# Pinning the modulation's products on VectorE and loading their rows one place ahead

## The chip, the cores and the metric

The kernel runs on one core of a Trainium2 chip. The metric is device time in microseconds (us): the median of three runs, and beside it one profiled execution from which all rows below come. Engines: TensorE (PE, matrix products; PEld its weight loads), VectorE (DVE), ScalarE (ACT), GpSimd (POOL) and SyncE (SP), whose queue issues the loads.

## The reference

Two layers of a hybrid trunk. 384 tokens (128 of a context pass, 256 of a denoising step) of width 1024 go through the same weights; each group has its own modulation vector. Per layer:

```
m   = silu(cvec) @ w_ada + b_ada            # 9 rows of 1024: shift, scale, gate for 3 sub-layers
ffn: h = rms_norm(x) * (1 + scale) + shift
     x = x + 0.5 * gate * ((silu(h @ wg) * (h @ wu)) @ wd)        # d_ff 2816
mixer: four head groups (windowed attention, a gated scan, latent attention, pooling) on one input
     projection, one output projection, x = x + gate * (...)
ffn again
```

A last rms_norm over x is the output y. All is float32.

## The kernel before, in words

The tokens lie along the free axis: x is eight tiles of 128 x 384 (k = 0 to 7). Every float32 weight tile is split into a high and a low half (`split_w`, L196 to L202): ScalarE copies the rounded high half (`higu`, `hidn`), VectorE subtracts it and leaves the low half (`logu`, `lodn`). A product is three TensorE instructions (`mm3`, L207 to L212): high weights with the high half of the input, high weights with its low half, and third, low weights with its high half. So TensorE needs the low half of a weight tile from its third instruction on.

An ffn (`ffn`, L299) goes through 38 places in a fixed order: 11 gate-and-up places (numbers 0 to 10; 48 products, or 24 for the gate and 24 for the up columns), 8 down places (11 to 18; 33 products each: 18 with the first 768 columns, 15 with the other 640), and the same again for the second half of d_ff (19 to 29, 30 to 37). At the end of a gate-and-up place VectorE multiplies `u` (gate times up, L336) and leaves its low half `al`; at the end of a down place it adds the result into x (`add_x`, L294, two instructions, one for each token group) and, in the second half, prepares the next sub-layer (`scaled`, L262, low half `hl`). The PSUM tag "d" has two banks, so x or u of a place must be read before the next but one can begin. Weights come by `load_w` (L121 to L125) into a pool of five buffers of 512 KB ("raw"): a load waits until a buffer's reader is done, and SyncE issues its loads in order.

The modulation rows are work on the side. The table SIDE says in which places a row n of layer l is worked out; a row is eight units (k = 0 to 7), spread over its places, so that where it has fewer places than units some places take two. Most run on VectorE (`ada_dve`, L167): a unit loads 512 KB of w_adaT and multiplies it in four instructions of 128 x 512 with the two modulation vectors, each leaving a sum (`accum_out`; the product itself goes to a PSUM tile named junk and is never read). One row (layer 0, n = 2) runs on TensorE (`ada_pe`, L143), in places 4 to 9 of the first ffn. `f()` of `side` (L1061) steps these generators once per place, behind the place's own code.

The code does not fix the order on an engine: a scheduler sets it from data dependences and its own estimates, and may move an instruction ahead of others. `tc.keep_in_program_order` pins one: it stays behind all that the program has before it on that engine, while later instructions that are not pinned may still move ahead of it. Each engine then executes its list in order.

At the end, `Sumsq` (L225) holds the sum of squares: with `apart` the last k is kept out of the running sum and added by a second product on TensorE; Ln and Exp on ScalarE make rstd, VectorE makes y and SyncE sends it (L1100 to L1107).

Of the kernel before, what the change touches and what calls it, by code (L numbers as in the profile page):

```python
# [7 lines left out]
F32 = mybir.dt.float32  # L8
F32R = mybir.dt.float32r
U8 = mybir.dt.uint8  # L10
AF = mybir.ActivationFunctionType
ALU = mybir.AluOpType
# [3 lines left out]
P = 128  # L16
D = 1024
KD = D // P
TP, TS = 128, 256
T = TP + TS  # L20
# [24 lines left out]
def trunk(ctx, tc, a):  # L45
    nc = tc.nc
# [8 lines left out]
    def nm(s):  # L55
        cnt[0] += 1
        return f"{s}_{cnt[0]}"
# [5 lines left out]
    def bank(s):  # L63
        return ps.tile([P, 512], F32, tag="b", name=nm(s), bufs=2)
# [4 lines left out]
    def xbank(s):  # L69
        return ps.tile([P, 2, 512], F32, tag="xb", name=nm(s), bufs=1)  # L70
# [50 lines left out]
    def load_w(src, s):  # L121
        t = sb.tile([P, 1024], F32, tag="raw", name=nm("raw" + s), bufs=5)
        n = src.shape[-1]
        nc.sync.dma_start(out=t[:, :n], in_=src)
        return t[:, :n]  # L125
# [29 lines left out]
    requests = {}  # L155
# [11 lines left out]
    def ada_dve(l, n):  # L167

        sums = sb.tile([P, KD, 2, 2], F32, tag="adasum", name=nm("adasum"), bufs=2)
        for k in range(KD):  # L170
            t = load_w(a["w_adaT"][l, n, k], "ada")
            for v in range(2):
                for z in range(2):
                    V.scalar_tensor_tensor(xbank("junk")[:, 0, :], t[:, z * 512:(z + 1) * 512], 1.0, requests[v, z],  # L174
                                           op0=ALU.mult, op1=ALU.mult, accum_out=sums[:, k, v, z:z + 1])
            if k == KD - 1:
                m = mods[l][:, n * 8:(n + 1) * 8, :]
                V.tensor_tensor(m, sums[:, :, :, 0], sums[:, :, :, 1], op=ALU.add)
                V.tensor_tensor(m, m, bada[:, l, n * 8:(n + 1) * 8].unsqueeze(2).to_broadcast([P, KD, 2]), op=ALU.add)
            yield  # L180
# [35 lines left out]
        V.tensor_tensor(lo, src, hi, op=ALU.subtract)  # L216


    def rstd_of(dst, acc, n):

        S.activation(dst, acc, AF.Ln, bias=epsb, scale=1.0 / n)
        S.activation(dst, dst, AF.Exp, scale=-0.5)
        return dst

    class Sumsq:  # L225
# [5 lines left out]
        def add(self, k):  # L231
            if self.n == 0:
                self.acc = one("ssq")
                S.activation(self.acc, x[k], AF.Square)
            else:
                sq = one("sq")
                S.activation(sq, x[k], AF.Square)  # L237
                if self.n < KD - self.apart:
                    (V if self.n == KD - 1 else G).tensor_tensor(self.acc, self.acc, sq, op=ALU.add)  # L239
                self.last = sq  # L240
            self.n += 1

        def end(self):
            b = bank("ms")
            PE.matmul(b[:, :T], ones, self.acc, start=True, stop=not self.apart)
            if self.apart:
                PE.matmul(b[:, :T], ones, self.last, start=False, stop=True)
            return rstd_of(sb.tile([P, T], F32, tag="rstd", name=nm("rstd"), bufs=1), b[:, :T], D)

    def log_exp():  # L250
        tc.keep_in_program_order(S.preload_act_table_set(LOGEXP))
# [39 lines left out]
                                   op0=ALU.add, op1=ALU.subtract)  # L291
        return t[:, 0, :], t[:, 1, :]

    def add_x(k, b, gt):  # L294
        for g, cs in GROUPS:
            V.scalar_tensor_tensor(x[k][:, cs], b[:, cs], gt[:, k, g:g + 1], x[k][:, cs], op0=ALU.mult, op1=ALU.add)  # L296


    def ffn(l, i, rstd, ab, nxt, side, hook=None, given=(), h=None):  # L299


        side = side()
        gt = None
        ssq = Sumsq(int(l == NL - 1 and i == 1))
        h = [None] * KD if h is None else h

        for half in range(2):
            act = []
            for fi in range(HF):
                f = half * HF + fi  # L310
                early = f < (5 if given else 4)
                order = [(z, k) for z in range(2) for k in range(KD)]
                if f < len(given):
                    (bg, bu), order = given[f], []
                else:
                    w = [weights(a["w_gu"][l, i, f, :, z * D:(z + 1) * D], "gu") for z in range(2)]
                    bg, bu = dbank("g"), dbank("u")
                if f == 0:
                    order.sort(key=lambda zk: zk[1])
                for z, k in order:  # L320
                    mm3((bg, bu)[z][:, :NX if early else T], w[z], k * P,
                        (hh[:, k, :], hl[:, k, :]) if early else h[k], k == 0, k == KD - 1)
                g, u = one("g"), one("u")
                if early:
                    sh = tiny("s", "sh", 2)
                    normed(g, bg, rstd, AF.Silu)
                    V.tensor_copy(sh, bu[:, T:NX])
                    V.tensor_tensor(u, bu[:, :T], rstd, op=ALU.mult)
                    for q, cs in GROUPS:
                        V.scalar_tensor_tensor(u[:, cs], u[:, cs], sh[:, q:q + 1], g[:, cs], op0=ALU.add, op1=ALU.mult)  # L330
                    for k in range((2 if given else f) * KD // 4, (f + 1) * KD // 4):
                        if k < KD and h[k] is None:
                            h[k] = hidden(k, ab, rstd)
                else:
                    S.activation(g, bg[:, :T], AF.Silu)  # L335
                    V.tensor_tensor(u, g, bu[:, :T], op=ALU.mult)  # L336
                if fi % 2 == 0:
                    ah = slot("H", "ah", (2, T), dt=F32R)
                    al = slot("H", "al", (2, T), dt=F32R)
                act.append((ah[:, fi % 2, :], al[:, fi % 2, :]))  # L340
                split_act(u, *act[-1])
                if f == NF - 1:
                    log_exp()
                if hook and f == 6:
                    hook()
                side()
            if gt is None:
                gt = gate(l, 2 * i)
            for j in range(KD):
                b = dbank("dn")  # L350
                fi = 0
                for z, n in ((0, 6), (1, 5)):
                    src = a["w_dn"][l, i, half, j]
                    w = weights(src[:, :6 * P] if z == 0 else src[:, 6 * P:], "dn")
                    for o in range(n):
                        mm3(b[:, :T], w, o * P, act[fi], fi == 0, fi == HF - 1)
                        fi += 1
                add_x(j, b, gt)
                if half == 1:
                    nxt(j)  # L360
                    ssq.add(j)
                side()
        return ssq
# [684 lines left out]
    def side(units):  # L1048

        places = [[] for _ in range(NF + 2 * KD)]  # L1050
        for by, l, n, p0, p1 in units:
            g = (ada_pe if by == "PE" else ada_dve)(l, n)
            for k in range(KD):
                places[p0 + k * (p1 + 1 - p0) // KD].append(g)
            if by == "PE":
                places[p1 + 1].append(g)
        first = min([NF] + [u[3] for u in units if u[0] == "DVE"])
        places[max(first - 2, 0)].insert(0, requests_of())
        todo = iter(places)

        def f():  # L1061
            for g in next(todo):
                next(g)
        return f
# [3 lines left out]
    def coefs_of(l, s):  # L1068
        if (l, s) not in coefs:
            coefs[l, s] = coef(l, s)  # L1070
        return coefs[l, s]

    def before(l, s):

        def f(j):
            if l < NL:
                at, bt = coefs_of(l, s)
                if j == 0:
                    shift(bt)
                scaled(j, at)  # L1080
        return f
# [7 lines left out]
    for l in range(NL):  # L1089
        if l > 0:  # L1090
            rstd = ssq.end()
            act_table(AF.Silu)
            ssq = ffn(l, 0, rstd, coefs_of(l, 0), before(l, 1), lambda: side(SIDE[2]))
        gt = gate(l, 1)
        rstd = ssq.end()
        act_table(AF.Sigmoid)
        ssq = mixers(l, rstd, gt, coefs_of(l, 1), before(l, 2))
        rstd = ssq.end()
        act_table(AF.Silu)
        ssq = ffn(l, 1, rstd, coefs_of(l, 2), before(l + 1, 0), lambda: side(SIDE[2 * l + 1]))  # L1100
    rstd = ssq.end()
    for k in range(KD):
        if k % 2 == 0:
            y = slot("M", "y", (2, T))
        V.scalar_tensor_tensor(y[:, k % 2, :], x[k], fnorm[:, k:k + 1], rstd, op0=ALU.mult, op1=ALU.mult)
        if k % 2 == 1:
            nc.sync.dma_start(out=a["o_y"][:, k - 1:k + 1, :], in_=y)  # L1107


_OUTS = {  # L1110
# [146 lines left out]
```

## Time and profile before

| | |
|---|---|
| median of 3 runs | 1548.63 us (1545.83 to 1549.92) |
| profiled execution | 1549.54 us, span 1547.8 us |
| TensorE busy | 1508.8 us, 97% |
| VectorE busy | 1177.6 us, 76% |
| modulation products on VectorE | 480, 339.8 us |
| bytes moved | 257.34 MB |

The span runs from the first instruction to the last. Products on TensorE are pipelined: they start 0.17 us apart while each lasts 0.34. "Idle before" is the time in which an engine did nothing before an instruction, and the arrow names what ended it. The granted clock of a stretch is 1.00 where TensorE had 2.4 GHz all through it and 0.50 at 1.2 GHz.

### The profile page before, as it was taken

To read this page: it belongs to the slowest core of one execution; us is meant where nothing else is said; L and a number is where in the kernel's file an instruction comes from. 1 tells how busy PE (TensorE), PEld (TensorE's weight loads), DVE (VectorE), ACT (ScalarE), POOL (GpSimd) and SP (SyncE) were. 2 spreads that over 40 slices of the span, in tenths; PEclk is the share of its full clock that TensorE was granted. 3 is DMA by queue.
4 is the path that set the end of the run, shared out by engine and by line. 5 is a ranking of instruction groups with operands and counts; after the bars stand their busy time and mean duration, and the time that the engine had idled before them with its cause. 6 is when DMAs were issued, how large, how long until landed. Compare 5 with 4: busy or idle time off the path is not lost.

```text
span 1547.8 us, 26740 instructions
## 1 busy us (share of the span) xinstructions
PE 1508.8 (97%) x10120; PEld 1426.4 (92%) x10120; DVE 1177.6 (76%) x2633; ACT 765.9 (49%) x1373; POOL 98.6 (6%) x122
## 2 busy tenths in 40 slices
PE   7999999999999999999999999999999999999997
PEld 5999999997778999999989999999877799999996
DVE  5889999969947988987977798785896599444433
ACT  6732333456788732333465323345677875323331
POOL 1000000101311000000100000001014010000001
PEclk9999999999999999999999999999999999999998
DMA  9777765642134465765654576555221156444331
GB/s 371 267 243 226 249 224 192 211 143 61 44 104 148 160 199 185 244 222 173 194 161 157 178 233 228 179 168 163 80 64 54 61 176 196 124 146 146 112 102 61
DMA packets 83026, 257.34 MB, mean 166 GB/s; under 512 B 9680, under 2 KB 11184, under 8 KB 82512
## 3 DMA queue, kind: packets, MB, share of 16 engines
q1 hardware_dynamic: 81744, 254.14, 50.5%
q8 instruction: 80, 1.31, 0.3%
q0 software_dynamic: 1152, 1.48, 0.3%
q14 instruction: 50, 0.41, 0.1%
HBM read 252.53 MB, written 2.26 MB: 165 GB/s over the span
## 4 chain that ended last, share of the span: by engine, by line
PE 70%; DVE 17%; DMA 6%; issue 3%; ACT 3%; SPq 0%; DVEq 0%; ACTq 0%
PE u L210 20%; PE g L210 19%; PE dn L210 12%; PE in L210 8%; DVE junk L174 5%; PE out L210 3%; DMA rawada<-in_w_adaT 3%; DVE lodn L201 2%; DMA rawgu<-in_w_gu 2%; DVE logu L201 2%; PE po L430 1%; DVE x L296 1%; PE sc L397 1%; DVE hl L265 1%; PE first L210 1%
## 5 line engine op out<-in xcount | busy, mean ns | idle before, releaser
L174 DVE SCALAR_TENSOR_TENSOR junk<-rawada,req 128x512 f32<-128x512 f32 x480 | 339.8, 708 | 31.1 <-DMA rawada<-in_w_adaT 20.9
L200 ACT ACTIVATE higu<-rawgu 128x1024 fp32r<-128x1024 f32 (+1 forms) x178 | 186.5, 1050 | 314.2 <-PE u L210 106.5
L210 PE MATMUL g<-h,higu 128*128 128x384 f32 x1136 | 291.6, 336 | 2.3 <-ACT g L335 2.2
L210 PE MATMUL u<-h,higu 128*128 128x384 f32 x1136 | 289.3, 334 | 2.3 <-DVE x L296 2.2
L201 DVE TENSOR_TENSOR logu<-rawgu,higu 128x1024 fp32r<-128x1024 f32 (+1 forms) x178 | 215.5, 1211 | 39.4 <-PE g L210 23.6
L210 PE MATMUL dn<-ah,hidn 128*128 128x384 f32 x704 | 236.1, 335 | 0.4 <-ACT hh L264 0.4
L210 PE MATMUL dn<-al,hidn 128*128 128x384 f32 x704 | 236.0, 335 | 0.0
L210 PE MATMUL dn<-ah,lodn 128*128 128x384 f32 x704 | 236.0, 335 | 0.0
L200 ACT ACTIVATE hidn<-rawdn 128x768 fp32r<-128x768 f32 (+1 forms) x128 | 101.3, 792 | 253.7 <-PE dn L210 70.1
L210 PEld LDWEIGHTS g<-h,higu 128*128 128x128 f32 x1136 | 205.7, 189 | 6.4 <-ACT g L335 3.1
L210 PEld LDWEIGHTS u<-h,higu 128*128 128x128 f32 x1136 | 204.9, 188 | 3.3 <-issue 1.5
L210 PE MATMUL g<-h,logu 128*128 128x384 f32 x568 | 190.6, 335 | 0.0
L210 PE MATMUL u<-h,logu 128*128 128x384 f32 x568 | 189.8, 334 | 0.0
L201 DVE TENSOR_TENSOR lodn<-rawdn,hidn 128x768 fp32r<-128x768 f32 (+1 forms) x128 | 113.4, 886 | 30.4 <-issue 17.0
L210 PEld LDWEIGHTS dn<-ah,hidn 128*128 128x128 f32 x704 | 132.1, 188 | 0.7 <-ACT hh L264 0.7
L210 PEld LDWEIGHTS dn<-ah,lodn 128*128 128x128 f32 x704 | 132.1, 188 | 0.0
L210 PEld LDWEIGHTS dn<-al,hidn 128*128 128x128 f32 x704 | 132.1, 188 | 0.0
L239 POOL TENSOR_TENSOR ssq<-ssq,sq 128x384 f32<-128x384 f32 x42 | 46.3, 1102 | 1155.5 <-ACT sq L237 658.0
L336 DVE TENSOR_TENSOR u<-g,u 128x384 f32<-128x384 f32 x71 | 39.2, 552 | 91.5 <-PE u L210 91.5
L210 PE MATMUL in<-hh,hiin 128*128 128x386 f32 x304 | 107.7, 354 | 0.0
L210 PEld LDWEIGHTS g<-h,logu 128*128 128x128 f32 x568 | 107.1, 189 | 0.0
L210 PEld LDWEIGHTS u<-h,logu 128*128 128x128 f32 x568 | 106.6, 188 | 0.0
(316 smaller groups left out, 2509.6 us busy)
## 6 DMA issues: line engine op xcount, KB each, us to landing
rawgu<-in_w_gu SPq DMA_DIRECT2D x170, 512.0 KB, 4.2
rawada<-in_w_adaT SPq DMA_DIRECT2D x120, 512.0 KB, 3.7
rawdn<-in_w_dn SPq DMA_DIRECT2D x64, 384.0 KB, 3.5
rawdn<-in_w_dn SPq DMA_DIRECT2D x64, 320.0 KB, 2.9
rawin<-in_w_in SPq DMA_DIRECT2D x38, 512.0 KB, 3.6
rawout<-in_w_out SPq DMA_DIRECT2D x32, 256.0 KB, 2.6
ada<-in_w_ada SPq DMA_DIRECT2D x16, 384.0 KB, 7.2
rawada<-in_w_ada SPq DMA_DIRECT2D x8, 512.0 KB, 4.9
```

What stands on the lines that cost most here:

```text
L174: V.scalar_tensor_tensor(xbank("junk")[:, 0, :], t[:, z * 512:(z + 1) * 512], 1.0, requests[v, z], op0=ALU.mult, op1=ALU.mult, accum_out=s ...
L200: S.activation(hi, raw, AF.Copy)
L201: V.tensor_tensor(lo, raw, hi, op=ALU.subtract)
L210: i = PE.matmul(out, wt, xt, start=first and n == 0, stop=last and n == 2)
L239: (V if self.n == KD - 1 else G).tensor_tensor(self.acc, self.acc, sq, op=ALU.add)
L265: V.scalar_tensor_tensor(hl[:, k, cs], x[k][:, cs], at[:, k, g:g + 1], hh[:, k, cs], op0=ALU.mult, op1=ALU.subtract)
L296: V.scalar_tensor_tensor(x[k][:, cs], b[:, cs], gt[:, k, g:g + 1], x[k][:, cs], op0=ALU.mult, op1=ALU.add)
L336: V.tensor_tensor(u, g, bu[:, :T], op=ALU.mult)
L397: PE.matmul(sc[:, u, :nk], q_of(u, blk), k_of(u, blk), start=True, stop=True)
L430: PE.matmul(bo[64 * u:64 * u + 64, :P], v_of(u, kt), pt[:, u, i * P:(i + 1) * P], start=(i == 0), stop=(i == len(kts) - 1))
```

## The change

In `ada_dve` the four products of a unit are pinned, and the load of unit k + 1 is issued in the code of unit k; the first unit issues two loads. At the end of the kernel the last x, its square, the sum, Ln, Exp and the first pair of y are worked out by column groups, 256 columns first and then 128, with Ln and Exp pinned; y takes its tiles from another pool, and its transfers go out on the queues of SyncE and ScalarE in turn, the last pair as two single tiles.

```diff
--- before.py
+++ after.py
@@ -167,12 +167,15 @@
     def ada_dve(l, n):
 
         sums = sb.tile([P, KD, 2, 2], F32, tag="adasum", name=nm("adasum"), bufs=2)
+        loads = [load_w(a["w_adaT"][l, n, 0], "ada")]
         for k in range(KD):
-            t = load_w(a["w_adaT"][l, n, k], "ada")
+            if k + 1 < KD:
+                loads.append(load_w(a["w_adaT"][l, n, k + 1], "ada"))
+            t = loads[k]
             for v in range(2):
                 for z in range(2):
-                    V.scalar_tensor_tensor(xbank("junk")[:, 0, :], t[:, z * 512:(z + 1) * 512], 1.0, requests[v, z],
-                                           op0=ALU.mult, op1=ALU.mult, accum_out=sums[:, k, v, z:z + 1])
+                    tc.keep_in_program_order(V.scalar_tensor_tensor(xbank("junk")[:, 0, :], t[:, z * 512:(z + 1) * 512], 1.0, requests[v, z],
+                                           op0=ALU.mult, op1=ALU.mult, accum_out=sums[:, k, v, z:z + 1]))
             if k == KD - 1:
                 m = mods[l][:, n * 8:(n + 1) * 8, :]
                 V.tensor_tensor(m, sums[:, :, :, 0], sums[:, :, :, 1], op=ALU.add)
@@ -216,10 +219,11 @@
         V.tensor_tensor(lo, src, hi, op=ALU.subtract)
 
 
-    def rstd_of(dst, acc, n):
-
-        S.activation(dst, acc, AF.Ln, bias=epsb, scale=1.0 / n)
-        S.activation(dst, dst, AF.Exp, scale=-0.5)
+    def rstd_of(dst, acc, n, pinned=False):
+
+        keep = tc.keep_in_program_order if pinned else lambda i: i
+        keep(S.activation(dst, acc, AF.Ln, bias=epsb, scale=1.0 / n))
+        keep(S.activation(dst, dst, AF.Exp, scale=-0.5))
         return dst
 
     class Sumsq:
@@ -234,18 +238,24 @@
                 S.activation(self.acc, x[k], AF.Square)
             else:
                 sq = one("sq")
-                S.activation(sq, x[k], AF.Square)
+                for _, cs in reversed(GROUPS) if self.apart and self.n == KD - 1 else ((0, slice(0, T)),):
+                    S.activation(sq[:, cs], x[k][:, cs], AF.Square)
                 if self.n < KD - self.apart:
                     (V if self.n == KD - 1 else G).tensor_tensor(self.acc, self.acc, sq, op=ALU.add)
                 self.last = sq
             self.n += 1
 
         def end(self):
-            b = bank("ms")
-            PE.matmul(b[:, :T], ones, self.acc, start=True, stop=not self.apart)
-            if self.apart:
-                PE.matmul(b[:, :T], ones, self.last, start=False, stop=True)
-            return rstd_of(sb.tile([P, T], F32, tag="rstd", name=nm("rstd"), bufs=1), b[:, :T], D)
+            rstd = sb.tile([P, T], F32, tag="rstd", name=nm("rstd"), bufs=1)
+            groups = GROUPS[::-1] if self.apart else ((0, slice(0, T)),)
+            bs = [bank("ms") for _ in groups]
+            for b, (_, cs) in zip(bs, groups):
+                PE.matmul(b[:, cs], ones, self.acc[:, cs], start=True, stop=not self.apart)
+            for b, (_, cs) in zip(bs, groups):
+                if self.apart:
+                    PE.matmul(b[:, cs], ones, self.last[:, cs], start=False, stop=True)
+                rstd_of(rstd[:, cs], b[:, cs], D, self.apart)
+            return rstd
 
     def log_exp():
         tc.keep_in_program_order(S.preload_act_table_set(LOGEXP))
@@ -291,8 +301,8 @@
                                    op0=ALU.add, op1=ALU.subtract)
         return t[:, 0, :], t[:, 1, :]
 
-    def add_x(k, b, gt):
-        for g, cs in GROUPS:
+    def add_x(k, b, gt, order=GROUPS):
+        for g, cs in order:
             V.scalar_tensor_tensor(x[k][:, cs], b[:, cs], gt[:, k, g:g + 1], x[k][:, cs], op0=ALU.mult, op1=ALU.add)
 
 
@@ -355,7 +365,7 @@
                     for o in range(n):
                         mm3(b[:, :T], w, o * P, act[fi], fi == 0, fi == HF - 1)
                         fi += 1
-                add_x(j, b, gt)
+                add_x(j, b, gt, GROUPS[::-1] if ssq.apart and half == 1 and j == KD - 1 else GROUPS)
                 if half == 1:
                     nxt(j)
                     ssq.add(j)
@@ -1098,13 +1108,17 @@
         rstd = ssq.end()
         act_table(AF.Silu)
         ssq = ffn(l, 1, rstd, coefs_of(l, 2), before(l + 1, 0), lambda: side(SIDE[2 * l + 1]))
+
     rstd = ssq.end()
-    for k in range(KD):
-        if k % 2 == 0:
-            y = slot("M", "y", (2, T))
-        V.scalar_tensor_tensor(y[:, k % 2, :], x[k], fnorm[:, k:k + 1], rstd, op0=ALU.mult, op1=ALU.mult)
-        if k % 2 == 1:
-            nc.sync.dma_start(out=a["o_y"][:, k - 1:k + 1, :], in_=y)
+    y = [slot("H", "y", (2, T)) for _ in range(KD // 2)]
+    for n, cs in ((0, GROUPS[1][1]), (0, GROUPS[0][1]), *((n, slice(0, T)) for n in range(1, KD // 2))):
+        for k in (2 * n, 2 * n + 1):
+            V.scalar_tensor_tensor(y[n][:, k % 2, cs], x[k][:, cs], fnorm[:, k:k + 1], rstd[:, cs],
+                                   op0=ALU.mult, op1=ALU.mult)
+            if n == KD // 2 - 1:
+                (nc.scalar, nc.sync)[k % 2].dma_start(out=a["o_y"][:, k, :], in_=y[n][:, k % 2, :])
+        if n < KD // 2 - 1:
+            (nc.sync, nc.scalar)[n % 2].dma_start(out=a["o_y"][:, 2 * n:2 * n + 2, cs], in_=y[n][:, :, cs])
 
 
 _OUTS = {
```

What the scheduler made of it is shown at two places. The first is VectorE in the first down-projection of layer 0 (places 11 to 18). `x<-dn_...` is the addition of a down place's result, `lodn` the low half of down weights, `junk` a modulation product. Before, from x of place 11 on; `lodn_1555` is the first low half of place 14, and `x<-dn_1422` is x of place 12:

```order
L296 SCALAR_TENSOR_TENSOR x<-dn_1364,G_1362,x 128x128
L296 SCALAR_TENSOR_TENSOR x<-dn_1364,G_1362,x 128x256
L201 TENSOR_TENSOR lodn_1510<-rawdn_1507,hidn_1509 128x640
L174 SCALAR_TENSOR_TENSOR junk_1545,adasum_1530<-rawada_1541,req_898 128x512
L174 SCALAR_TENSOR_TENSOR junk_1547,adasum_1530<-rawada_1541,req_901 128x512
L201 TENSOR_TENSOR lodn_1555<-rawdn_1552,hidn_1554 128x768
L174 SCALAR_TENSOR_TENSOR junk_1549,adasum_1530<-rawada_1541,req_904 128x512
L174 SCALAR_TENSOR_TENSOR junk_1601,adasum_1530<-rawada_1599,req_895 128x512
L174 SCALAR_TENSOR_TENSOR junk_1603,adasum_1530<-rawada_1599,req_898 128x512
L296 SCALAR_TENSOR_TENSOR x<-dn_1422,G_1362,x 128x128
L296 SCALAR_TENSOR_TENSOR x<-dn_1422,G_1362,x 128x256
L201 TENSOR_TENSOR lodn_1579<-rawdn_1576,hidn_1578 128x640
```

After, from x of place 13 on; `lodn_1557` and `lodn_1581` are the two low halves of place 14:

```order
L306 SCALAR_TENSOR_TENSOR x<-dn_1482,G_1364,x 128x128
L306 SCALAR_TENSOR_TENSOR x<-dn_1482,G_1364,x 128x256
L177 SCALAR_TENSOR_TENSOR junk_1535,adasum_1530<-rawada_1531,req_895 128x512
L204 TENSOR_TENSOR lodn_1557<-rawdn_1554,hidn_1556 128x768
L177 SCALAR_TENSOR_TENSOR junk_1537,adasum_1530<-rawada_1531,req_898 128x512
L204 TENSOR_TENSOR lodn_1581<-rawdn_1578,hidn_1580 128x640
```

The first low half of place 14 stood ahead of x of place 12; it now stands behind x of place 13, with a product between.

The second is SyncE's queue at the first modulation row on VectorE, in place 7 of the first ffn, with the semaphores that each load waits for. `rawada` are modulation rows (from w_adaT for VectorE, from w_ada for TensorE), `rawgu` gate and up weights, here those of place 8. Before:

```order
L124 DMA rawada_1064<-in_w_adaT 128x1024 [waits DMAHW6_49,DMAHW2_49,DVE_49]
L515 DMA ka_3338<-in_kcT 128x128
L516 DMA va_3339<-in_vc 128x128 [waits DMAHW4_49]
L124 DMA rawada_1074<-in_w_adaT 128x1024 [waits DMAHW5_49,DMAHW0_49,DVE_49]
L124 DMA rawada_1084<-in_w_ada 128x1024 [waits PE_49]
L124 DMA rawada_1090<-in_w_ada 128x1024 [waits DMAHW7_49,DMAHW1_49,DVE_49]
L576 DMA ckv_3792<-in_ckvT 128x128
L582 DMA kr_3908<-in_krT 32x128
L124 DMA rawgu_1096<-in_w_gu 128x1024 [waits DMAHW2_49,DVE_49]
L124 DMA rawgu_1102<-in_w_gu 128x1024 [waits DMAHW5_49,DMAHW3_49,DVE_49]
```

After:

```order
L124 DMA rawada_1064<-in_w_adaT 128x1024 [waits DMAHW6_49,DMAHW2_49,DVE_49]
L525 DMA ka_3338<-in_kcT 128x128
L526 DMA va_3339<-in_vc 128x128 [waits DMAHW4_49]
L124 DMA rawada_1066<-in_w_adaT 128x1024 [waits DMAHW5_49,DMAHW0_49,DVE_49]
L124 DMA rawada_1076<-in_w_adaT 128x1024 [waits PE_49]
L124 DMA rawada_1086<-in_w_ada 128x1024 [waits DMAHW7_49,DMAHW1_49,DVE_49]
L586 DMA ckv_3792<-in_ckvT 128x128
L592 DMA kr_3908<-in_krT 32x128
L124 DMA rawada_1092<-in_w_ada 128x1024 [waits DMAHW2_49,PE_49]
L124 DMA rawgu_1098<-in_w_gu 128x1024 [waits DMAHW7_49,DMAHW3_49,PE_49]
L124 DMA rawgu_1104<-in_w_gu 128x1024 [waits DMAHW4_49,DMAHW2_49,PE_49]
```

Between `rawgu_1001` of place 7 and the weights of place 8 stood four modulation rows, and now five; the gate weights of place 8 waited for VectorE and now wait for TensorE. TensorE's list there, after, from the end of place 7's up-product on (`ada` are its modulation products, `g` the gate of place 8):

```order
L213 MATMUL u_1008<-h_727,higu_1003 128x384 x2
L213 MATMUL u_1008<-h_727,logu_1004 128x384
L149 MATMUL ada_814<-rawada_1086,cpad 32x256 x4
L149 MATMUL ada_814<-rawada_1092,cpad 32x256 x4
L213 MATMUL g_1110<-h_386,higu_1100 128x384 x2
L213 MATMUL g_1110<-h_386,logu_1101 128x384
```

The products that read `rawada_1086` and `rawada_1092` stand behind place 7's last up-product and right ahead of place 8.

## Rows read from the trace of the kernel before

**Rows 1.** The page, busy time of each engine, share of the span, instructions.
```profile
PE 1508.8 (97%) x10120; PEld 1426.4 (92%) x10120; DVE 1177.6 (76%) x2633; ACT 765.9 (49%) x1373; POOL 98.6 (6%) x122
```
**Rows 2.** TensorE in order of time: start, us, instruction, idle before and its releaser.
```profile
175.65 0.59 PE L210 MATMUL u<-h,higu 128*128 128x384 f32 x2 [1.17 <-DVE x L296]
...
647.28 0.59 PE L210 MATMUL u<-h,higu 128*128 128x384 f32 x2 [1.03 <-DVE x L296]
...
785.02 0.41 PE L210 MATMUL u<-hh,higu 128*128 128x386 f32 x1 [2.63 <-ACT hh L264]
...
935.31 0.64 PE L210 MATMUL g<-h,higu 128*128 128x384 f32 x2 [1.82 <-ACT g L335]
```
**Rows 3.** Stretches: length, busy us of PE, PEld, DVE, ACT, POOL, clock, DMA share, GB/s.
```profile
785.00:789.00 4.00, 3.98 (x14) 4.00 (x15) 2.13 (x4) 0.83 (x2) 0.00 (x0) 0.57 0.77 248
...
935.50:939.50 4.00, 4.00 (x15) 4.00 (x15) 3.90 (x11) 1.59 (x2) 0.00 (x0) 0.57 0.75 208
...
172.00:177.00 5.00, 3.83 (x23) 3.54 (x22) 4.96 (x12) 1.26 (x2) 0.00 (x0) 1.00 0.76 256
```
**Rows 4.** The chain that ended last, by time: start, us, what.
```profile
926.99 6.73 DMA rawgu<-in_w_gu
...
935.31 6.00 PE g L210 x24
941.31 4.16 PE u L210 x24
...
1352.77 45.76 PE dn L210 x264
```
**Rows 5.** VectorE in order of time, in a down-projection.
```profile
913.48 0.95 DVE L201 TENSOR_TENSOR lodn<-rawdn,hidn 128x768 fp32r<-128x768 f32 x1
914.35 0.69 DVE L174 SCALAR_TENSOR_TENSOR junk<-rawada,req 128x512 f32<-128x512 f32 x1
914.96 0.14 DVE L174 DVE_READ_ACCUMULATOR junk<-rawada,req 128x1 f32 x1
915.14 0.70 DVE L174 SCALAR_TENSOR_TENSOR junk<-rawada,req 128x512 f32<-128x512 f32 x1
...
916.55 0.74 DVE L296 SCALAR_TENSOR_TENSOR x<-dn,G,x 128x128 f32<-128x128 f32 x2
917.20 0.82 DVE L201 TENSOR_TENSOR lodn<-rawdn,hidn 128x640 fp32r<-128x640 f32 x1
...
923.32 1.22 DVE L201 TENSOR_TENSOR logu<-rawgu,higu 128x1024 fp32r<-128x1024 f32 x1
924.46 0.70 DVE L174 SCALAR_TENSOR_TENSOR junk<-rawada,req 128x512 f32<-128x512 f32 x1
```
**Rows 6.** DMA issues: count, KB each, median us from issue to landing.
```profile
rawgu<-in_w_gu SPq DMA_DIRECT2D x170, 512.0 KB, 4.2
...
rawdn<-in_w_dn SPq DMA_DIRECT2D x64, 384.0 KB, 3.5
...
o_y<-y SPq DMA_DIRECT2D x4, 384.0 KB, 2.8
```
**Rows 7.** The page, costliest groups: busy us, mean ns of one, idle before.
```profile
L200 ACT ACTIVATE higu<-rawgu 128x1024 fp32r<-128x1024 f32 (+1 forms) x178 | 186.5, 1050 | 314.2 <-PE u L210 106.5
```
**Rows 8.** Who waited for whom: us in total, times, longest.
```profile
DVE junk L174 <- DMA rawada<-in_w_adaT: 20.9, 23, 2.8
```
**Rows 9.** All engines in order of time, the last 12 us.
```profile
1535.85 0.74 DVE L296 SCALAR_TENSOR_TENSOR x<-dn,G,x 128x128 f32<-128x128 f32 x2 [4.98 <-PE dn L210]
1536.68 0.52 ACT L237 ACTIVATE sq<-x 128x384 f32<-128x384 f32 x1 [5.19 <-DVE x L296]
...
1538.21 0.58 ACT L221 ACTIVATE rstd<-ms,epsb 128x384 f32<-128x384 f32 x1 [1.00 <-PE ms L247]
...
1539.38 4.32 DVE L1105 SCALAR_TENSOR_TENSOR y<-x,c_later,rstd 128x384 f32<-128x384 f32 x8 [2.79 <-ACT rstd L222]
```

## The prediction

> **What bounds the kernel now.** I read the page's busy shares first. TensorE is busy 1508.8 of 1547.8 us, VectorE 1177.6 [rows 1]: TensorE sets the time, and all its gaps together are 39 us, so there is little to win and much to lose. Next come TensorE's gaps in order of time. Four of them follow from VectorE being late [rows 2]: 1.17 us at 175.65 and 1.03 at 647.28 (the up-product waits until x has been read out of its PSUM bank), 2.63 at 785.02, 1.82 at 935.31. The rest lies at the start, in the mixers and in the last 12 us. The stretches around two of these gaps show something more [rows 3]: behind the waits of 2.63 and 1.82 us the granted clock falls to 0.57 of a 4 us stretch, so part of it ran at 1.2 GHz instead of 2.4, while around the wait of 1.17 us it stays at 1.00. The chain of waits prices it: the 24 products behind the 1.82 us wait took 6.00 us, the next 24 took 4.16 [rows 4]. The clock costs 1.84 us on top of such a wait. Half a down-projection, 264 products, took 45.76 us [rows 4], so a down place takes 5.72.
>
> Last, VectorE's own rows [rows 5]. From start to start: one modulation product 0.79 us (914.35 to 915.14, with its accumulator read), so a unit of four 3.16; a low half of 768 down columns 0.87; of 1024 gate or up columns 1.14; the two pieces of x together 0.65.
>
> **The change, part by part.** The pin. The number of instructions stays, 480 products; their place changes. Before, they ran as soon as their row was there, up to two places early, and both low halves of a place stood ahead of the x of the place in front. After, a unit may not run ahead of its own place's u, al, x and hl, and x waits for TensorE's last product of that place. What stands behind x on VectorE therefore starts only when TensorE has already run out of everything but the first two products of the next place (they need the high half alone). Where the low half of the next place stands behind x, TensorE must wait: VectorE starts x about as late as TensorE takes for those two products, so the wait is about the sum of what VectorE does from x to the end of that low half. In the order before there is no such place. I count eleven after:
> - ffn 1 of layer 0, down places 14 and 15: x, one product, low half, 0.65 + 0.79 + 0.87 = 2.31 each; place 18: x, two products, low half, 0.65 + 1.58 + 0.87 = 3.10. Together 7.7.
> - its second half, place 32: x and low half, 1.52; place 33: x, a product, half of hl (0.33, taken as x's, the columns are the same) and low half, 2.64. Together 4.2.
> - ffn 2 of layer 0: place 16 as 18 above, 3.10; place 19 (gate again): x, two products, a gate low half, 0.65 + 1.58 + 1.14 = 3.37, less two more products that need high halves alone (0.35), 3.0; place 33: x, four products, hl, low half, 0.65 + 3.16 + 0.65 + 0.87 = 5.3. Together 11.4.
> - ffn 1 of layer 1: places 13 and 16, 3.10 each, and 19, 3.0. Together 9.2.
>
> The rows one place ahead. A unit that starts with two k in its first place now issues three loads at once, and there are five raw buffers. In place 7 of the very first ffn three rows for VectorE and two for TensorE fill all five, and the gate weights of place 8 wait for TensorE's own modulation products, which stand behind place 7's last up-product. So the transfer begins when TensorE has nothing left: 4.2 us to landing [rows 6], the high half on ScalarE 1.05 [rows 7], the low half 1.14, less 0.35 for the two products that need the high half alone: 6.0 us. With the longest such transfer of the chain of waits, 6.73 us [rows 4], it is 8.6. VectorE by itself would be done a little sooner there (u, al, five products and the low half). In the Trainium skill, "Perfetto Trace Analysis", section "Identifying Performance Opportunities", a gap that repeats on the engine that should be full can mean too few buffers for the next tile; it speaks against loading ahead into the same five buffers. Before, TensorE waits nowhere here for a weight buffer, so no row of before shows it.
>
> Sum of these waits: 7.7 + 4.2 + 11.4 + 9.2 + 6.0 = 38.5 us. A second way to the same size: in a down place with two units VectorE has 6.32 + 1.74 + 0.65 = 8.7 us of work against TensorE's 5.72, 3.0 too many; before, hoisting spread it over the gate places; ten down places have two units, 30 us, and 6.0 for place 8 make 36. VectorE can also come late to x itself where it is still busy with products when TensorE ends: between 0 and 10 us (a third of the 30); I take 4, since most stretches between the waits fit into 5.72.
>
> The clock. Of the twelve waits, place 8 among them, all but one (1.52) are 2.3 us or more. The two of before that were 1.82 or more were each followed by the slow stretch, those of 1.2 or less were not. Bounds: 0, and 11 x 1.84 = 20 us. I take nine, 16.6 us, because places 14 and 15, and 32 and 33, follow each other so closely that the stretches may fall together.
>
> What goes. The waits at 175.65 and 647.28 with the small gap behind the first, 1.5 + 1.0; the one at 935.31 with its clock, 1.82 + 1.84 = 3.7 (another takes its place, counted above); of the one at 785.02 with its clock, 4.5, I take 2, since x of the last down place is there still followed by a low half. Together 8.2, between 4 and 11. The 20.9 us that products waited for their rows [rows 8] go as well, but TensorE did not wait behind them: nothing.
>
> The tail. Before: x at 1535.85, its square at 1536.68, Ln at 1538.21, first y at 1539.38, eight y in 4.32 us to 1543.70, last transfer 2.8 us to landing [rows 6, 9]. After, 256 columns go first through x, square, sum, Ln and Exp; each step loses some 0.1 to 0.25 us of its duration and the 128 columns follow beside it. First y about 0.9 us sooner; ten y instead of eight cost 0.25 more; the last transfer is half as large and goes out on one of two queues. Between 0 and -1.5; I take -0.9.
>
> Sum on the profiled execution: 1549.5 + 38.5 + 4 + 16.6 - 8.2 - 0.9 = 1599.5. The median of the three runs is 0.9 below the profiled one: 1599.
>
> **Rivals.**
> - The waits come, the clock stays up (VectorE's arrears are worked off in the waits, and most end under 1.8 us): 1599 - 16.6 = 1582. For it: only two waits of before show the fall. Against it: both do.
> - Starved buffers everywhere, not in place 8 alone. Each late low half frees its raw buffer late, and SyncE issues in order: the next weights then cost transfer and high half again. Eight more places with 3.5 us of that: 1627. For it: three rows are loaded at once wherever a unit begins with two k. Against it: on SyncE's queue most of these loads still stand far enough ahead of their use.
> - Faster. With rows a place ahead, products would find their data, and with the pin u, al and x would never stand behind them; the waits at [rows 2] go and nothing replaces them: 1549 - 8.2 - 0.9 = 1540. It decides where VectorE reaches each low half before TensorE has finished the place in front. In the Trainium skill, "Trainium Kernel Development and Optimization", section "Best Practices", transfers are to be overlapped with computing by double buffering, which is what loading ahead does; the trace gives it 20.9 us of VectorE's idle time to work on. Against it: the data dependence leaves no way round the eleven places.
> - The waits come but are shorter, because VectorE's pinned products slip further behind than the places say, and the tail and the removed waits pay for them: within 0.3%.
>
> **How the numbers follow.** Forecast as summed 0.52, clock stays up 0.25, starved buffers 0.15, faster 0.05, no change 0.03. Range: low, no clock stretch, all 11 us of old waits gone and the tail at -1.5, 1549 + 38.5 - 12.5 = 1575, less 7 for waits partly hidden, 1568; high, 1549 + 38.5 + 10 + 20 + 2.6 - 4 = 1616, and up to 1630 for starved buffers. 0.3% (4.6 us) is about what a measurement here can tell from no change. Faster 0.05, same 0.03, slower 0.92.
>
> **What would show it.** Right: TensorE's waits for the low halves (lodn, logu) of VectorE, none of which stands in its list before, with some 30 us; a gap of 5 to 9 us near 100 us behind which stands a transfer of rawgu; granted clock 0.5 behind the larger gaps; VectorE's waits for rawada nearly gone; ffn 2 of layer 1, which has but one unit, unchanged. Wrong: down places of 5.72 us throughout, or TensorE's gaps unchanged in sum.

## The result and the profile after

The changed kernel takes 1644.33 us (median of four runs, 1643.48 to 1646.15) against 1548.68 before: a ratio of 1.063, interval 1.0615 to 1.0644. It is 95.6 us slower. The direction was forecast; the size was not, and 1644 lies above the range (1568 to 1630).

The page's busy times of the changed kernel, which answer to [rows 1]:

```profile
PE 1549.9 (94%) x10124; PEld 1446.1 (88%) x10124; DVE 1188.5 (72%) x2635; ACT 769.3 (47%) x1376; POOL 104.6 (6%) x122
```

TensorE stands idle for 1641.7 - 1549.9 = 91.8 us, before for 39.0: 52.8 us more. For almost the same number of products it is busy 41.1 us longer, so they also ran slower. VectorE is busy for about as long as before. Its work did not grow; it is done at another time.

Whom TensorE waited for in the changed kernel, summed over the span (us in total, times, longest), where before neither `lodn`, `logu`, `hidn` nor `higu` was ever waited for:

```profile
PE dn L213 <- DVE lodn L204: 28.4, 23, 5.0
PE dn L213 <- ACT hidn L203: 14.3, 14, 2.3
PE g L213 <- ACT higu L203: 8.1, 4, 4.7
...
PE u L213 <- ACT higu L203: 3.9, 3, 2.1
PE g L213 <- ACT g L345: 3.4, 5, 1.3
PE g L213 <- DVE logu L204: 3.0, 7, 0.7
```

Low halves: 28.4 + 3.0 = 31.4 us. High halves: 14.3 + 8.1 + 3.9 = 26.3. The second sum is the surprise. A high half needs nothing from VectorE, only its weights. Why it is late shows in one place. All engines of the changed kernel in order of time, in the first down-projection (places 12 to 14 of the prediction):

```profile
142.66 4.59 SPq L124 DMA_DIRECT2D rawada<-in_w_adaT  x3
...
145.88 0.35 DVE L306 SCALAR_TENSOR_TENSOR x<-dn,G,x 128x128 f32<-128x128 f32 x1
146.15 0.69 DVE L177 SCALAR_TENSOR_TENSOR junk<-rawada,req 128x512 f32<-128x512 f32 x1
...
146.75 0.48 DVE L306 SCALAR_TENSOR_TENSOR x<-dn,G,x 128x256 f32<-128x256 f32 x1
147.15 0.69 DVE L177 SCALAR_TENSOR_TENSOR junk<-rawada,req 128x512 f32<-128x512 f32 x1
...
147.76 0.82 DVE L204 TENSOR_TENSOR lodn<-rawdn,hidn 128x640 fp32r<-128x640 f32 x1
...
148.60 2.58 SPq L124 DMA_DIRECT2D rawdn<-in_w_dn  x2
...
150.86 0.34 PE L213 MATMUL dn<-ah,lodn 128*128 128x384 f32 x1
...
152.56 0.84 ACT L203 ACTIVATE hidn<-rawdn 128x768 fp32r<-128x768 f32 x1 [6.87 <-DMA rawdn<-in_w_dn]
...
153.43 0.96 DVE L204 TENSOR_TENSOR lodn<-rawdn,hidn 128x768 fp32r<-128x768 f32 x1 [0.20 <-ACT hidn L203]
153.45 0.45 PE L213 MATMUL dn<-ah,hidn 128*128 128x384 f32 x1 [2.25 <-ACT hidn L203]
153.74 0.34 PE L213 MATMUL dn<-al,hidn 128*128 128x384 f32 x1
...
154.45 0.44 PE L213 MATMUL dn<-ah,lodn 128*128 128x384 f32 x1 [0.37 <-DVE lodn L204]
```

Read it from the bottom. TensorE starts a place at 153.45, 2.25 us late, because the high half was copied only at 152.56; ScalarE had been idle for 6.87 us, waiting for the transfer. That transfer was issued at 148.60. Ahead of it SyncE issued three row loads over 4.59 us, and then it waited for a buffer: the low half at 147.76 had to read its raw tile first, and it stood behind x and pinned products. The low half of the late tile then costs only 0.37 us more. So the line runs from VectorE's order over the raw buffer and SyncE's queue to the weights, and comes back to VectorE.

The clock. Cores view, span and mean granted clock, of the kernel before and of the changed one:

```profile
core 0: 1547.8 us, clock 0.995
```
```profile
core 0: 1641.7 us, clock 0.981
```

What is missing to 1.00 is 1.9% of 1641.7 = 31.2 us, before 0.5% of 1547.8 = 7.7 (0.005 is rounded): 23.5 us more. That is an estimate, since the mean also counts time in which TensorE is idle. Stretches of the changed kernel, columns as in [rows 3]:

```profile
101.50:108.30 6.80, 5.30 (x15) 4.80 (x16) 5.59 (x12) 2.12 (x2) 0.00 (x0) 0.50 0.75 230
153.00:157.00 4.00, 3.18 (x16) 2.85 (x17) 3.81 (x10) 1.14 (x2) 0.00 (x0) 1.00 0.38 140
162.90:166.30 3.40, 3.40 (x11) 3.40 (x12) 2.61 (x7) 0.11 (x1) 0.00 (x0) 0.51 0.77 245
```

The first stands behind the starved gate weights of place 8, the second behind the 2.25 us above, the third behind two waits of 1.0 us in a row:

```profile
161.19 0.45 PE L213 MATMUL dn<-ah,hidn 128*128 128x384 f32 x1 [1.00 <-ACT hidn L203]
...
162.79 0.57 PE L213 MATMUL dn<-ah,lodn 128*128 128x384 f32 x1 [0.98 <-DVE lodn L204]
```

VectorE's idle time before the products, before 31.1 us (20.9 of them for rows, [rows 8]) and now 8.5, and the last x and the first y, answering to [rows 9]:

```profile
L174 DVE SCALAR_TENSOR_TENSOR junk<-rawada,req 128x512 f32<-128x512 f32 x480 | 339.8, 708 | 31.1 <-DMA rawada<-in_w_adaT 20.9
```
```profile
L177 DVE SCALAR_TENSOR_TENSOR junk<-rawada,req 128x512 f32<-128x512 f32 x480 | 340.6, 710 | 8.5
```
```profile
1630.91 0.74 DVE L306 SCALAR_TENSOR_TENSOR x<-dn,G,x 128x256 f32<-128x256 f32 x2 [4.98 <-PE dn L213]
...
1633.65 4.58 DVE L1116 SCALAR_TENSOR_TENSOR y<-x,c_later,rstd 128x256 f32<-128x256 f32 x10 [2.00 <-ACT rstd L226]
```

Rows did arrive earlier, and TensorE gained nothing by it. From the last x to the end of the span: 10.8 us, before 11.95. The final chain is 1.15 us shorter.

### The profile page after: what moved, and what is told of

Same layout as the page of the kernel before. It is cut to its first block, busy times and chain, and to the rows that moved or that the text cites. A ratio compares the mean times of both kernels' runs of the same rounds, so it can differ in the third digit from the quotient of the medians.

```text
span 1641.7 us, 26680 instructions
## 1 busy us (share of the span) xinstructions
PE 1549.9 (94%) x10124; PEld 1446.1 (88%) x10124; DVE 1188.5 (72%) x2635; ACT 769.3 (47%) x1376; POOL 104.6 (6%) x122
## 4 chain that ended last, share of the span: by engine, by line
PE 54%; DVE 23%; DMA 13%; ACT 6%; issue 4%; SPq 0%; ACTq 0%; DVEq 0%
PE g L213 12%; PE u L213 12%; PE dn L213 11%; DVE junk L177 10%; PE in L213 8%; DMA rawgu<-in_w_gu 8%; DMA rawdn<-in_w_dn 5%; DVE logu L204 3%; PE out L213 3%; DVE lodn L204 3%; ACT higu L203 2%; PE sc L407 1%; PE po L440 1%; DVE hl L275 1%; DVE x L306 1%
## 5 line engine op out<-in xcount | busy, mean ns | idle before, releaser
L213 PE MATMUL g<-h,higu 128*128 128x384 f32 x1136 | 296.8, 341 | 11.5 <-ACT higu L203 8.1
L213 PE MATMUL dn<-ah,lodn 128*128 128x384 f32 x704 | 246.5, 350 | 28.5 <-DVE lodn L204 28.4
L213 PE MATMUL dn<-ah,hidn 128*128 128x384 f32 x704 | 245.0, 348 | 15.8 <-ACT hidn L203 14.3
L213 PE MATMUL dn<-al,hidn 128*128 128x384 f32 x704 | 242.9, 345 | 0.4 <-DVE al L219 0.4
L213 PE MATMUL g<-h,logu 128*128 128x384 f32 x568 | 194.5, 342 | 3.2 <-DVE logu L204 3.0
L213 PEld LDWEIGHTS dn<-ah,lodn 128*128 128x128 f32 x704 | 137.2, 195 | 37.3 <-DVE lodn L204 37.2
L213 PEld LDWEIGHTS dn<-ah,hidn 128*128 128x128 f32 x704 | 137.3, 195 | 21.9 <-ACT hidn L203 21.9
L213 PEld LDWEIGHTS dn<-al,hidn 128*128 128x128 f32 x704 | 137.0, 195 | 0.9 <-DVE al L219 0.9
L244 POOL TENSOR_TENSOR ssq<-ssq,sq 128x384 f32<-128x384 f32 x42 | 52.0, 1237 | 1244.3 <-ACT sq L242 1244.2
L213 PE MATMUL in<-hh,loin 128*128 128x386 f32 x304 | 106.3, 350 | 0.0
```

The source lines that it names most:

```text
L213: i = PE.matmul(out, wt, xt, start=first and n == 0, stop=last and n == 2)
```

## The experiments

The theory of the prediction is A: the pin puts x and products in front of the next low half. The rival B: the five raw buffers are too few for rows that are held longer, and late low halves are a consequence. B1, B2, C and D below divide B.

**One part at a time.** Code cuts that end in `...` are shortened. `e_tail` has only the final chain of the change (its lines in `Sumsq`, `rstd_of`, `add_x` and at the end), `e_ahead` only the loads, `e_pin` only the pin. The last two against the kernel before:

```diff
 e_ahead
-            t = load_w(a["w_adaT"][l, n, k], "ada")
+            if k + 1 < KD:
+                loads.append(load_w(a["w_adaT"][l, n, k + 1], "ada"))
+            t = loads[k]
 e_pin
-                    V.scalar_tensor_tensor(xbank("junk")[:, 0, :], ...
+                    tc.keep_in_program_order(V.scalar_tensor_tensor(xbank("junk")[:, 0, :], ...
```

> Only the final chain by column groups; products and row loads as before. Both theories: nothing changes up to the last x. From the last x to the end of the span before takes 11.95 us (1535.85 to 1547.8), the changed kernel 10.8 (1630.91 to 1641.7). So 1.0 to 1.2 us less than before, about 1547.6, within 0.3% of it. If the column groups cost as much as they win, 1548.7.

Measured 1546.67 against 1547.61, ratio 0.9992 (0.998 to 1.0004): no difference that can be told. In its trace the time from the last x to the end is 10.8 us, as expected.

> Only the rows one place ahead; products not pinned, old final chain. Theory A (the pin puts low halves behind x; buffers matter in place 8 alone): VectorE can work products off early and give the raw buffers back, no low half stands behind x of the place in front; 1549, within 3 us, and TensorE's waits for high halves under 2 us in sum. Theory B (five raw buffers are too few for rows held a place longer): the rows starve the weights also without the pin; high-half waits of 10 us or more, 1565 or more.

Measured 1544.87, ratio 0.9982 (0.997 to 0.9994): slightly faster. Rows loaded ahead starve nothing as long as VectorE may work them off when they land. B as worded here is refuted. The gain of 2.7 us does not come from rows that are there sooner: VectorE waits 26.1 us for them, 20.9 before.

> Only the pin; rows loaded in the code of their own unit, old final chain. Theory A: the waits for low halves stay as in the changed kernel, 31 us of TensorE's idle time, with the clock stretches that follow them; only the waits for high halves (27 us) go: 1549 + 31 + 15 = about 1595. Theory B: pin and loads ahead need each other, since a pinned product gives its buffer back late and a load ahead takes it early; low halves are late because their weights come late. Then the pin alone costs less than half of the 95.6 us: under 1590, nearer 1575, and waits for low halves fall too, to 20 us or less.

Measured 1581.74, ratio 1.022 (1.0196 to 1.0244): 34 us, a little over a third of the whole. TensorE's waits in it:

```profile
PE dn L210 <- DVE lodn L201: 8.6, 12, 1.6
...
PE dn L210 <- ACT hidn L200: 4.1, 7, 1.2
PE u L210 <- DVE u L336: 4.1, 3, 2.3
PE g L210 <- DVE logu L201: 3.4, 6, 1.1
```

Low halves cost 12.0 us here, not 31. The same products are pinned in the same places; only the loads moved. A is too simple: most of the low-half waits come from pin and loading ahead together.

**Buffers of their own.** In `e_slots` the changed kernel keeps pin, loading ahead and final chain, and rows leave the raw pool:

```diff
+    def load_row(l, n, k):
+        ts = []
+        for z in range(2):
+            t = slot("S", "rawada", (512,))
+            nc.sync.dma_start(out=t, in_=a["w_adaT"][l, n, k, :, z * 512:(z + 1) * 512])
+            ts.append(t)
+        return ts
...
-        loads = [load_w(a["w_adaT"][l, n, 0], "ada")]
+        loads = [load_row(l, n, 0)]
...
-                loads.append(load_w(a["w_adaT"][l, n, k + 1], "ada"))
+                loads.append(load_row(l, n, k + 1))
...
-                    tc.keep_in_program_order(V.scalar_tensor_tensor(xbank("junk")[:, 0, :], t[:, z * 512:(z + 1) * 512], ...
+                    tc.keep_in_program_order(V.scalar_tensor_tensor(xbank("junk")[:, 0, :], t[z], ...
```

> The changed kernel, but each modulation row is loaded as two tiles of 128 x 512 into four buffers that lie free during the ffn, so that all five raw buffers belong to weights. Pin, loading ahead and final chain stay. Theory A: products still stand where they are pinned and VectorE has as much to do between x and the next low half: the low-half waits (31 us) and their clock stay, the high-half waits go: about 1600. Theory B: with buffers of their own the rows no longer hold up the weights, weights land early, and the low halves can stand ahead of x of the place in front: TensorE's waits for low and high halves both under 5 us, 1540 to 1550.

Measured 1549.46, ratio 1.0012 (1.0002 to 1.0022). 95 us are gone, with the pin in place. TensorE waits for no low half and no high half; the longest list entries are others:

```profile
PE ada L978 <- DMA ada<-in_w_ada: 7.2, 3, 5.1
PE u L221 <- DVE x L314: 4.7, 3, 3.7
PE po L448 <- ACT pt L444: 4.3, 6, 1.2
```

VectorE, SyncE and one copy of ScalarE in `e_slots`, in the same down-projection:

```profile
140.62 1.81 SPq L124 DMA_DIRECT2D rawdn<-in_w_dn  x2
141.13 0.95 DVE L212 TENSOR_TENSOR lodn<-rawdn,hidn 128x768 fp32r<-128x768 f32 x1
...
142.65 0.85 ACT L211 ACTIVATE hidn<-rawdn 128x768 fp32r<-128x768 f32 x1 [1.83 <-PE dn L221]
...
143.40 0.35 DVE L314 SCALAR_TENSOR_TENSOR x<-dn,G,x 128x128 f32<-128x128 f32 x1
...
144.83 0.82 DVE L212 TENSOR_TENSOR lodn<-rawdn,hidn 128x640 fp32r<-128x640 f32 x1
145.68 1.81 SPq L124 DMA_DIRECT2D rawdn<-in_w_dn  x2
...
146.18 0.95 DVE L212 TENSOR_TENSOR lodn<-rawdn,hidn 128x768 fp32r<-128x768 f32 x1
...
149.40 0.34 DVE L314 SCALAR_TENSOR_TENSOR x<-dn,G,x 128x128 f32<-128x128 f32 x1
```

The low half of the next place's first tile (146.18) stands ahead of x (149.40) in spite of the pin. The weights are there in time: ScalarE's idle time before the high half (142.65) is ended by TensorE and no longer by a transfer. My reading, which no run isolates, is that the scheduler puts a low half where it expects its tile, so that with weights early it needs no place behind x. What is shown is that the order that I had taken for a consequence of the pin goes with the buffers. One thing changes beside them: a row now comes as two transfers of 256 KB and two tiles. That was not tried inside the shared pool. Two of the next four runs change the number of buffers without it.

**Number or sharing.** `e_pin_raw4` is the pin alone with `bufs=4` for the raw pool; `e_slots_raw3` is `e_slots` with `bufs=3`, as many bytes as the five shared buffers; `e_pin_slots` is the pin alone with rows in buffers of their own; `e_raw4` is the kernel before with `bufs=4`.

```diff
 e_pin_raw4, e_raw4 (e_slots_raw3: bufs=3)
-        t = sb.tile([P, 1024], F32, tag="raw", name=nm("raw" + s), bufs=5)
+        t = sb.tile([P, 1024], F32, tag="raw", name=nm("raw" + s), bufs=4)
 e_pin_slots (load_row, the pin and t[z] as above)
-            t = load_w(a["w_adaT"][l, n, k], "ada")
+            t = load_row(l, n, k)
```

> The kernel before with the pin alone, and four raw buffers instead of five; rows not loaded ahead, old final chain. Theory B1 (a row loaded one place ahead does harm because it holds one raw buffer a place longer): pin with four buffers is then the same as pin with loads ahead and five; 1640, within 15 us, with TensorE's idle time before low and before high halves near the 31 and 27 us of the changed kernel. Theory B2 (it is the place of the row loads in SyncE's queue, ahead of the next weights, that does harm, not their number): with loads in their own unit again it stays near the pin alone, 1582 to 1600.

Measured 1656.11, ratio 1.0696 (1.0672 to 1.0719). Its waits are nearly those of the changed kernel:

```profile
PE dn L210 <- DVE lodn L201: 27.6, 22, 4.9
PE dn L210 <- ACT hidn L200: 15.1, 18, 2.3
PE g L210 <- ACT higu L200: 8.5, 4, 4.7
...
PE g L210 <- DVE logu L201: 5.5, 11, 1.0
...
PE u L210 <- ACT higu L200: 4.2, 2, 2.5
```

That is 33.1 us for low halves and 27.8 for high ones, against 31.4 and 26.3. The time is 1 us above B1's range (up to 1655) and 56 above B2's. B1 fits and B2 does not: with the pin, loading one row ahead does much the same as one raw buffer less. Here rows come as one transfer each, so the number of buffers alone brings the low-half waits from 12.0 us (`e_pin`) to 33.1.

> The changed kernel with rows in buffers of their own (four of 128 x 512, two rows) and only three raw buffers, all for weights: as many bytes in all as the five that the changed kernel shares. Theory C (too few buffers in all): starved as the changed kernel, over 1600. Theory D (the sharing does it: a pinned row keeps a buffer that the weights of the next place wait for): 1545 to 1560, waits for low and high halves under 8 us in sum.

Measured 1562.82, ratio 1.0098 (1.0081 to 1.0116), a little above D's range and far from C's. Its waits for halves come to 1.3 us. As many bytes cost 95.6 us shared and 15 us apart.

> The kernel before with the pin alone and rows in buffers of their own, not loaded ahead, old final chain. If the shared buffers are the whole cost of the pin (34 us by itself): 1545 to 1553. If the pin by itself puts VectorE's products in front of x and low halves at a price: 1560 to 1580. Loading ahead has nothing to win in either case if this is within 3 us of the same kernel with loads ahead (1549.5).

Measured 1550.31, ratio 1.0019 (1.0008 to 1.0029): with buffers apart the pin costs 2 to 3 us (1.2 to 4.5 by the interval) instead of 34, and loading ahead has nothing to win on top (1549.46 with it).

> The kernel before with four raw buffers instead of five, and no other change: what one buffer less costs where the products are not pinned. Theory D (only a pinned row keeps its buffer until the end of its place): VectorE works a row off as soon as it lands and gives the buffer back; 1548 to 1560. Theory C (four are too few for these loads, pinned or not): over 1600, and the 108 us of pin with four buffers would not be the pin's.

Measured 1592.78, ratio 1.0293 (1.0272 to 1.0314). Neither range was hit: one buffer less costs 44.5 us without any pin. But it costs them in another way. In its trace TensorE waits for no low or high half, but above all for `u` (the longest item of its list), x and `hh`, which ScalarE makes from x, and VectorE for rows (the answer to [rows 8], 20.9 us before):

```profile
PE u L210 <- DVE u L336: 10.8, 15, 2.1
```
```profile
DVE junk L174 <- DMA rawada<-in_w_adaT: 91.1, 57, 3.3
```

I read it so: unpinned, a product stands early in VectorE's list and waits there for its row, with `u` and x behind it; pinned, it waits in its place and the weights are late. One buffer less costs time either way, and it is paid on different tiles. One buffer less and the pin cost 44.5 and 34 us apart and 108 together, more than the sum.

**Does the place in VectorE's list matter at all?** `e_front` is the changed kernel with the side's step moved ahead of `add_x` in the down places.

```diff
+                side()
                 add_x(j, b, gt, ...
                 if half == 1:
                     nxt(j)
                     ssq.add(j)
-                side()
```

> The changed kernel, with the side's step put ahead of the addition into x in the down places, so that pinned products stand in front of x of their own place and no longer behind it. Theory A (the prediction's reason: x, products and low half in one line behind TensorE's last product): only x and the low half, 1.52 us, still stand in that line; the low-half waits halve and the time is under 1605. Theory D (the shared buffers are held either way): 1640, within 20 us.

Measured 1617.9, ratio 1.0444 (1.0419 to 1.047). Between the two answers: it is 26 us faster than the changed kernel, and the waits for `lodn` are 20.5 us instead of 28.4:

```profile
PE dn L213 <- DVE lodn L204: 20.5, 18, 5.5
```

The edit does two things at once, taking products out of the line behind x and giving their raw buffers back sooner, so the 26 us are not all theory A's. A is a part, not the main one.

**A version that beats both.** The parts that did no harm, loading ahead and the final chain, without the pin (`e_best`), and the same with rows in buffers of their own (`e_best_slots`). Against the changed kernel and against `e_slots`:

```diff
-                    tc.keep_in_program_order(V.scalar_tensor_tensor(xbank("junk")[:, 0, :], ...
+                    V.scalar_tensor_tensor(xbank("junk")[:, 0, :], ...
```

> Rows one place ahead and the final chain by column groups, without the pin. The two measured apart gave 2.7 and 0.9 us less than before: if they add, 1544, a ratio of 0.9977. If the row loads ahead won by chance of the schedule and the new final chain moves it, 1547.

Measured 1544.92, ratio 0.9976 (0.9965 to 0.9987): 3.1 us less than before by the medians (2.0 to 5.4 by the interval). The parts may add as expected; the interval cannot tell their sum from loading ahead alone (2.7 us). TensorE is busy 1506.7 us of its span of 1543.2.

> Loads one place ahead, rows in buffers of their own, the final chain by column groups, no pin. If the 2.7 us of loading ahead come from shorter waits for row loads, buffers of their own let rows land still earlier: 1543 to 1545. If they come from weights that are due before rows in the shared buffers, they are lost: 1547 to 1550, as with the pin (1549.5).

Measured 1558.56, ratio 1.0074 (1.0055 to 1.0092): slower than either answer, and 9 us slower than the same kernel with the pin (`e_slots`). TensorE waits in it for VectorE's `u`:

```profile
PE u L221 <- DVE u L354: 5.5, 10, 1.2
```

With rows in buffers of their own the pin is worth something; in the shared pool it costs 34 us or more. And without the pin, buffers of their own lose 14 us against the shared pool (`e_best`). Why was not followed further.

## Why the prediction was wrong

**The place of the loss was right.** TensorE waits for low halves: forecast 32.5 us (38.5 less the 6.0 of place 8), measured 31.4. Some places came as counted: 2.71 us each before 964.86 and 987.92 in the first ffn of layer 1 (forecast 3.1), 4.96 us before 820.66 (forecast 5.3):

```profile
820.66 0.69 PE L213 MATMUL dn<-ah,lodn 128*128 128x384 f32 x1 [4.96 <-DVE lodn L204]
...
964.86 0.52 PE L213 MATMUL dn<-ah,lodn 128*128 128x384 f32 x1 [2.71 <-DVE lodn L204]
```

Others did not. In places 14 and 15, the first two of the count at 2.31 us each, TensorE waited 0.37 and 0.98 us for the low half, and before that 2.25 and 1.00 for the high half. In all there are 23 + 7 waits instead of 11, many of them under 1.1 us and in places that I had not counted. That the sum agrees is luck.

**The reason for it was not.** "The data dependence leaves no way round the eleven places" is refuted by `e_slots`: same pin, same products, and no wait at such a place. I had read the order of the changed kernel and laid it to the pin, when it goes with the buffers.

**The step that failed is the row loads, "the rows one place ahead".** I priced one starved transfer, place 8, at 6.0 us. It measured 4.65 us of idle time on TensorE, and 0.25 more for the low half. But high halves in all cost 26.3 us, 21.6 of them elsewhere, where the sum had nothing. The rival of starved buffers named exactly this and priced it well (28 us for eight more places); I gave it 0.15, on the ground that most loads still stand far enough ahead on SyncE's queue. The queue's order does not tell that: a load's start is set by the instruction that gives its buffer back, and that one stood late on VectorE.

The prediction also holds that, since TensorE did not wait for a weight buffer at place 8 before, no row of before shows such a wait. One did, at another place. The wait of 1.82 us at 935.31, which it counts among those that follow from VectorE being late, hangs on a late weight transfer. Between the transfer of 926.99 in [rows 4] and TensorE's start the chain of the kernel before has:

```profile
933.82 1.06 ACT higu L200
934.88 0.39 ACT g L335
```

The copy of the high half waited for the transfer, `g` stood behind it on ScalarE, and TensorE waited for `g`. So late weights already cost the kernel before 1.82 us, with a slow stretch behind it.

**The clock.** Forecast 16.6 us less the 1.84 that go behind 935.31, measured 23.5 more than before. The rule that I took from two waits (1.82 us and more are followed by the slow stretch, 1.2 and less are not) does not hold: two waits of 1.0 us in a row were followed by it, one of 2.25 us was not.

**What was left out.** Waits 31.4 + 26.3, clock 23.5, old waits gone -4.7 (29.0 to 24.3 us in the rest of TensorE's list of waits), final chain -1.2: 75.3. The profiled executions differ by 93.9. Some 9 us come from starting again: from 150.86 to 153.45 pass 2.59 us, of which 2.25 are shown as idle and 0.17 are the usual pitch; 0.17 is lost beside each of the 51 waits for halves. The next product comes 0.29 us later (153.45 to 153.74) instead of 0.17; at 0.12 for each of the 51 that is up to 6 us more. Both are estimates from this one place. About 4 us stay open. The 4 us for VectorE late at x were not found: TensorE waits 1.0 us for x, before 3.2.

**What was right.** The tail (-0.9 forecast, -1.2 measured; by itself too small to tell). VectorE's waits for rows went (31.1 us of idle time before products to 8.5) and gave nothing. The second ffn of layer 1, with one unit, shows no wait over 0.15 us between 1397.6 and 1631.2 us.

## What to carry to other kernels

A pool of buffers that work on the side shares with the main stream is a hidden order between them: ask of each side tile not when it is loaded but when it is given back, and which load of the main stream waits for that on its queue. Give such work buffers of its own before pinning it; here the same bytes cost 95.6 us shared and 15 us apart. This is not a rule for work that is not pinned: there the shared pool with loads ahead took 1544.92 us and buffers apart 1558.56. And when a scheduler's order has changed, find out which resource it answers to before laying it to the edit that one sees.

## What was not expected of the hardware

The granted clock does not follow the length of one wait: it was 1.00 in the 4 us behind a wait of 2.25 us (153.00 to 157.00) and 0.51 behind two waits of 1.0 us that ended 1.6 us apart (162.90 to 166.30). In `e_pin`, where no wait for a half is longer than 1.6 us, the mean is 0.995, as before. What decides it these runs do not show.
